# Another order of a recurrence's steps, with the second parts of its weights made on VectorE

## The chip, the cores and the metric

The kernel runs on one core of a Trainium2 chip. The core has TensorE (PE, matrix products; PEld is its loading of weights), VectorE (DVE), ScalarE (ACT), GpSimd (POOL) and SyncE (SP, which here issues DMAs), each with its own queue of instructions worked off in order. The metric is the device time of one execution in microseconds, the median of several runs.

## The reference

Two layers of a diffusion transformer on 512 latent and 256 context tokens (768 in all), width 1024. Layer 0 mixes by a gated linear recurrence, layer 1 by latent attention; each is followed by a SwiGLU feed-forward. The change lies in the mixer of layer 0:

```python
g, u = split(h @ w_in)                       # 1024 channels each
u = dwconv4(u) + b                           # along the tokens, one before and two after
for d, reverse in enumerate((False, True)):  # both directions
    r = sigmoid(blockdiag(u, gw[d, 0]) + gb[d, 0]);  i = sigmoid(blockdiag(u, gw[d, 1]) + gb[d, 1])
    a = exp(-8 * r * softplus(-lam[d]));  b = sqrt(1 - a**2) * (i * u)
    h_d = scan(a, b)                         # context first, then latent
x += mod * (((h_0 + h_1) * gelu(g)) @ w_out)
```

## The kernel before

Channels stand on the partitions and the 768 tokens along the free axis. Every float32 product is made of three rounded ones: `wh*xh`, `wh*xl` and `wl*xh`, where `wh` is the weight rounded and `wl` the rest (`mm3`, matmuls at L791).

The class `Stream` brings the weights. SP loads one into a `raw` buffer, of which there are two; ACT rounds it to `wh` (L108); a second instruction, here called its low, makes `wl = raw - wh` (L119) on the engine that `low_engine` names, which is GpSimd up to the end of the recurrence. A raw buffer comes free, and SP issues the next load, only after its last low. There are four `wh`/`wl` pairs. `done(i)` gives a pair back and calls `advance()`, which makes the lows still pending, splits the next unit, and leaves the low of the last one pending until the next `advance`, `flush` or `get` of that unit.

The recurrence goes through four blocks n of 256 channels, each in two halves. Its order is written by hand in `STEPS` (L296 to L304). Each step is a letter with n and further digits:

- `u`, `g`: input products (L791); `c`: convolution (ACT L895, six DVE instructions L899), then its split into `uh` (ACT L904) and `ul` (DVE L905); `G`: gelu (ACT L970).
- `t`, `T`: the two gate products of a direction and half (PE tiles `ga`) and their tanh (ACT L931).
- `e`: decays (DVE L941, three ACT instructions L948 to L950, DVE L951); `q`: square root (ACT L1037); `s`: the scan (DVE L956, then L958 and L959 forward, or L962 and the sum L964 backward).
- `m`: states times gelu (DVE L985), split into `mh` (ACT L986) and `ml` (DVE L988); `o`: an output tile (PE tiles `lo`) and its residual (DVE L767).
- `w`: `done` of the oldest used weight; `a`: a step of the modulation's products (PE `psada`, L570), whose DMAs POOL issues (L242).

The tiles `u`, `g`, `ga` and `lo` take turns in three PSUM buffers, so each of them waits until the tile three before it has been read. Names of steps carry digits: t201 is the gate product of block 2, direction 0, half 1. In the rows of the instruction order below, the tiles carry block, direction, half and gate: `ga2010` is t201, `ga2011` is T201, `lo2_4` is o24.

Of the kernel before, what the change touches and what calls it, by code (L numbers as in the profile page):

```python
# [145 lines left out]
def kernel(ctx, tc, x, c, ctx_in, c_ctx, ada_w, ada_b, norm_mix_g, norm_ffn_g, ffn_w_in,  # L146
# [3 lines left out]
    nc = tc.nc  # L150
    act, dve, pe = nc.scalar, nc.vector, nc.tensor
# [28 lines left out]
    def ps_main(name):  # L180
        return psstack[0][1].tile([P, 1024], F32, name=name, tag="main")
# [79 lines left out]
    st = Stream(nc, raw_pool, w_pool)  # L261
# [23 lines left out]
    def lru_gate_unit(n, d):  # L285
# [9 lines left out]

    STEPS = (  # L296
# [7 lines left out]
        "a g31 s311 w o20 o21 G30 o22 G31 w m3 w o23 o24 o25 o26 o27").split()  # L304

    g_units[0][0], = std_units(lru_w_in[0], 0, P)
    u_units[0] = [std_units(lru_w_in[0], D + i * P, P)[0] for i in range(2)]
# [200 lines left out]
    def ada_evac(wait=False):  # L508

        if ada_state["evac"] is None:  # L510
            return
        i, l, ch, sb = ada_state["evac"]
        if wait and ada_state["calls"] < 2:
            ada_state["calls"] += 1
            return
        ada_state["evac"] = None
        px = ps_aux(f"adax{i}")
        for cc in range(2):
            pe.transpose(px[:, cc * P:(cc + 1) * P], sb[:, cc * P:(cc + 1) * P], ident)

        order = "p (c j) -> p c j" if l and ch < 2 else "p (j c) -> p c j"
        n = dict(c=2, j=4)
        pv = px[:, :256].rearrange("p (c j r) -> p c j r", r=32, **n)
        for v in range(2):
            dve.tensor_tensor(mod[:, l, ch, v, :].rearrange(order, **n), pv[:, :, :, v],
                              adab(l, ch).rearrange(order, **n), op=ALU.add)
        if ch in (1, 4):
            w = l + (2 if ch == 4 else 0)
            for v in range(2):
                dve.scalar_tensor_tensor(gm[:, w, v, :], mod[:, l, ch, v, :], 1.0, gcol(w),  # L530
                                         op0=ALU.add, op1=ALU.mult)
# [12 lines left out]
    def ada_add():  # L544
        if ada_state["sums"] is None:
            return
        i, l, ch, half, total = ada_state["sums"]
        ada_state["sums"] = None
        if half == 0:
            ada_ps["half"] = psa.tile([P, 512], F32, name=f"psada{i}", tag="ada")  # L550
        ps = ada_ps["half"]
        for j in range(2):
            r = 64 * half + 32 * j
            pe.matmul(ps[r:r + 32, :256], pick[:, 0, :], total[:, j * 256:(j + 1) * 256], start=True, stop=True)
        if half == 1:
            ada_copy(i, l, ch, ps)
# [18 lines left out]
    def ada_one():  # L575
        ada_fill()
        i = ada_state["used"]
        l, ch, *f = adas[i]
        (ada_sum if l and ch > 1 else ada_product)(i, ada_tiles.pop(i), l, ch, *f)
        ada_state["used"] += 1  # L580
        ada_fill()

    def ada_step(n=1):

        if ada_state["sums"]:
            ada_state["calls"] += 1
            if ada_state["calls"] < 2:
                return
            ada_add()
        else:  # L590
            ada_evac(True)
        for _ in range(n):
            if ada_state["used"] < N_ADA[0] and not ada_state["sums"]:
                ada_one()
# [202 lines left out]
    def prod(ps, unit, xh, xl, parts, kt=KT, off=0, at=None):  # L797
        wh, wl = st.get(unit)
        for k in range(kt):
            if at and k in at:  # L800
                at[k]()
            mm3(ps, wk(wh, k), wk(wl, k), xh[:, k], xl[:, k], parts, k == 0, k == kt - 1, off)
# [118 lines left out]
    def gate(n, d, kk, g, uh, ul):  # L921

        wh, wl = st.get(gate_units[n][d])
        ps = ps_main(f"ga{n}{d}{kk}{g}")
        for k in range(2):
            o = (g * 2 + k) * 256 + kk * P
            mm3(ps, wh[:, o:o + P], wl[:, o:o + P], uh[:, k], ul[:, k], SL, k == 0, k == 1)
        tag, bufs = ("gel", 4) if (n, d, g) == (3, 1, 1) else (f"tg{g}", 4 - 2 * g)
        th = lt(f"tg{n}{d}{kk}{g}", tag, bufs)
        gi = (d * 2 + g) * 8 + 2 * n + kk  # L930
        act.activation(th, ps[:, :T], AF.Tanh, scale=0.5, bias=gbh[:, gi:gi + 1])  # L931
        gs["t", n, d, kk, g] = th
        if kk == g == 1:
            used.append(gate_units[n][d])

    def decay(n, d, kk, y):

        tr, ti = gs["t", n, d, kk, 0], gs["t", n, d, kk, 1]
        ci = d * 8 + 2 * n + kk
        cs = slice(ci, ci + 1)  # L940
        dve.scalar_tensor_tensor(ti, ti, 1.0, y, op0=ALU.add, op1=ALU.mult)  # L941
        if (n, d) == (3, 1):
            a = lt(f"a{n}{d}{kk}", "yc", 2)
        else:
            a = tmp.tile([P, T], F32, name=f"a{n}{d}{kk}", tag="nt")
        b = lt(f"b{n}{d}{kk}", "b", 1)
        gs["a", n, d, kk] = a
        act.activation(a, tr, AF.Exp, scale=m4[:, cs], bias=m4[:, cs])  # L948
        act.activation(b, tr, AF.Exp, scale=m8[:, cs], bias=m8[:, cs])
        act.activation(tr, tr, AF.Tanh, scale=p4[:, cs], bias=p4[:, cs])  # L950
        dve.scalar_tensor_tensor(tr, b, 1.0, tr, op0=ALU.add, op1=ALU.mult)  # L951

    def states(n, d, kk):

        a, b, ti = gs["a", n, d, kk], gs["t", n, d, kk, 0], gs["t", n, d, kk, 1]
        dve.tensor_tensor(b, b, ti, op=ALU.mult)  # L956
        if d == 0:
            dve.tensor_tensor_scan(b[:, CTXS], a[:, CTXS], b[:, CTXS], 0.0, op0=ALU.mult, op1=ALU.add)  # L958
            dve.tensor_tensor_scan(b[:, LAT], a[:, LAT], b[:, LAT], b[:, T - 1:T],  # L959
                                   op0=ALU.mult, op1=ALU.add)  # L960
        else:
            dve.tensor_tensor_scan(b[:, ::-1], a[:, ::-1], b[:, ::-1], 0.0, op0=ALU.mult, op1=ALU.add)  # L962
            f = gs["t", n, 0, kk, 0]
            dve.tensor_tensor(f, f, b, op=ALU.add)  # L964
# [3 lines left out]
    def gelu_of(n, kk, ps):  # L968
        ge = lt(f"gel{n}_{kk}", "gel", 4)
        act.activation(ge, ps[:, :T], AF.Gelu_apprx_tanh)  # L970
        gel[n, kk] = ge
        used.append(g_units[n][kk])
# [21 lines left out]
    def new_block(n):  # L994
        uc[n] = [lt(f"u{i}{n}", f"u{i}", 1, F32R, [P, 2, T]) for i in "hl"]
# [3 lines left out]
    def product(op, n, kk):  # L999
        pss[op, n, kk] = ps = ps_main(f"{op}{n}_{kk}")  # L1000
        prod(ps, (u_units if op == "u" else g_units)[n][kk], hh, hl, SL)

    def convolution(n, kk):
        ycs[n, kk] = conv(2 * n + kk, pss["u", n, kk])
        if kk == 0:
            new_block(n)
        conv_split(ycs[n, kk], *uc[n], kk)
        used.append(u_units[n][kk])

    new_block(0)  # L1010
    gelu_of(0, 0, p0[0])
    st.done(used.pop())
    ada_step()
# [6 lines left out]
    for op, *f in STEPS:  # L1020
        n, *f = map(int, f or "0")
        if op in "ug":
            product(op, n, *f)
        elif op == "c":
            convolution(n, *f)
        elif op == "G":
            gelu_of(n, *f, pss["g", n, *f])
        elif op in "tT":
            gate(n, *f, "tT".index(op), *uc[n])
        elif op == "w":  # L1030
            if used:
                st.done(used.pop(0))
        elif op == "e":
            decay(n, *f, ycs[n, f[1]])
        elif op == "q":
            b = gs["t", n, *f, 0]
            act.activation(b, b, AF.Sqrt, scale=0.25)  # L1037
        elif op == "s":
            states(n, *f)
        elif op == "m":  # L1040
            gated_states(n)
        elif op == "o":
            out_tile_of(n, *f, mts[n])
        else:
            ada_step()
    for i in used:
        st.done(i)
    ada_until(0, 5)
# [707 lines left out]
```

## Time and profile before

| | us |
|---|---|
| runs, median of 3 | 1565.74 (1564.92 to 1567.44) |
| profiled execution | 1566.9 |
| its span (first to last instruction) | 1565.1 |
| PE busy | 1510.2 (96%) |
| DVE, ACT, POOL busy | 936.8, 676.1, 260.3 |
| mean granted TensorE clock | 0.986 |

The span is what the profile covers; the profiled execution is 1.8 us longer than it. The recurrence lies between about 62 and 345 us. Lines are numbered as in the kernel before; a group of rows gives how many instructions it holds and their mean.

### The profile page before, as it was taken

To read this page: it belongs to the slowest core of one execution; us is meant where nothing else is said; L and a number is where in the kernel's file an instruction comes from. 1 tells how busy PE (TensorE), PEld (TensorE's weight loads), DVE (VectorE), ACT (ScalarE), POOL (GpSimd) and SP (SyncE) were. 2 spreads that over 40 slices of the span, in tenths; PEclk is the share of its full clock that TensorE was granted. 3 is DMA by queue.
4 is the path that set the end of the run, shared out by engine and by line. 5 is a ranking of instruction groups with operands and counts; after the bars stand their busy time and mean duration, and the time that the engine had idled before them with its cause. 6 is when DMAs were issued, how large, how long until landed. Compare 5 with 4: busy or idle time off the path is not lost.

```text
span 1565.1 us, 21623 instructions
## 1 busy us (share of the span) xinstructions
PE 1510.2 (96%) x8903; PEld 1320.1 (84%) x8903; DVE 936.8 (60%) x1407; ACT 676.1 (43%) x989; POOL 260.3 (17%) x251
## 2 busy tenths in 40 slices
PE   7999998979999999999999999999998999999998
PEld 5887876868879898999989887899998888888887
DVE  5765778687855666758677477665537543233234
ACT  5486555834323241433414344666644321232223
POOL 3223333252000101001010210111144100000002
PEclk8999999989999999999999999999999999999999
DMA  9334334131134334334332121110112432233222
GB/s 358 123 114 135 108 111 130 56 108 48 68 102 121 96 120 119 125 100 128 104 119 77 54 69 64 29 43 28 54 55 75 162 126 96 81 104 111 81 69 94
DMA packets 134995, 155.15 MB, mean 99 GB/s; under 512 B 6251, under 2 KB 112352, under 8 KB 134896
## 3 DMA queue, kind: packets, MB, share of 16 engines
q1 hardware_dynamic: 122272, 112.21, 22.1%
q0 software_dynamic: 12320, 41.02, 8.1%
q8 instruction: 70, 1.15, 0.3%
q10 hardware_dynamic: 304, 0.53, 0.1%
q14 instruction: 29, 0.24, 0.0%
HBM read 151.64 MB, written 2.10 MB: 98 GB/s over the span
## 4 chain that ended last, share of the span: by engine, by line
PE 83%; DVE 11%; ACT 4%; issue 1%; DMA 1%; SPq 0%; DVEq 0%; ACTq 0%
PE f L791 14%; PE fo L1212 12%; PE x L1166 10%; PE fo L791 8%; PE z L1166 5%; PE lo L791 3%; PE s L1553 3%; PE ga L791 2%; PE wo L791 2%; PE y L1166 2%; PE o L1595 2%; PE p L791 2%; PE g L791 2%; DVE yc L899 1%; PE t L1571 1%; DVE tg L962 1%
## 5 line engine op out<-in xcount | busy, mean ns | idle before, releaser
L108 ACT ACTIVATE wh<-raw 128x1024 fp32r<-128x1024 f32 (+3 forms) x247 | 208.4, 871 | 202.7 <-PE fo L1212 56.4
L119 POOL TENSOR_TENSOR wl<-raw,wh 128x1024 fp32r<-128x1024 f32 (+2 forms) x56 | 136.3, 2443 | 337.8 <-ACT wh L108 325.8
L119 DVE TENSOR_TENSOR wl<-raw,wh 128x1024 fp32r<-128x1024 f32 (+3 forms) x191 | 181.1, 961 | 18.7 <-ACT wh L108 18.5
L767 DVE SCALAR_TENSOR_TENSOR xT<-fo,mod,xT 128x512 f32<-128x512 f32 (+1 forms) x124 | 74.1, 626 | 127.6 <-PE fo L1212 64.6
L239 POOL DMA_DIRECT2D ada<-in_ada_w_dram x96 | 51.6, 537 | 465.4 <-PE psada L570 219.0
L791 PE MATMUL f<-hh,wh 128*128 128x512 f32 x320 | 124.7, 390 | 0.0
L791 PE MATMUL f<-hh,wl 128*128 128x512 f32 x320 | 124.5, 389 | 0.0
L791 PE MATMUL f<-hl,wh 128*128 128x512 f32 x320 | 124.5, 389 | 0.0
L785 POOL TENSOR_TENSOR acc<-acc,sq 128x256 f32<-128x256 f32 (+1 forms) x52 | 50.7, 974 | 381.0 <-ACT sq L783 379.9
L1212 PE MATMUL fo<-ah,wh 128*128 128x512 f32 (+1 forms) x352 | 98.3, 345 | 0.9 <-DVE g L1273 0.8
L1212 PE MATMUL fo<-al,wh 128*128 128x512 f32 (+1 forms) x352 | 95.8, 338 | 0.4 <-DVE al L1201 0.4
L1212 PE MATMUL fo<-ah,wl 128*128 128x512 f32 (+1 forms) x352 | 95.3, 337 | 0.0
L1109 DVE TENSOR_TENSOR sg<-sg,f 128x512 f32<-128x512 f32 x20 | 13.8, 688 | 116.3 <-ACT sg L1108 116.3
L1108 ACT ACTIVATE sg<-f 128x512 f32<-128x512 f32 x20 | 12.0, 599 | 147.9 <-PE f L791 147.9
L791 PE MATMUL fo<-ah,wh 128*128 128x512 f32 (+1 forms) x200 | 73.0, 365 | 0.0
L791 PE MATMUL fo<-ah,wl 128*128 128x512 f32 (+1 forms) x200 | 72.7, 364 | 0.0
L791 PE MATMUL fo<-al,wh 128*128 128x512 f32 (+1 forms) x200 | 72.7, 364 | 0.0
L791 PEld LDWEIGHTS f<-hh,wh 128*128 128x128 f32 x320 | 60.1, 188 | 13.3 <-issue 0.8
L791 PEld LDWEIGHTS f<-hh,wl 128*128 128x128 f32 x320 | 60.1, 188 | 12.4
L791 PEld LDWEIGHTS f<-hl,wh 128*128 128x128 f32 x320 | 60.1, 188 | 12.4
L1212 PEld LDWEIGHTS fo<-ah,wh 128*128 128x128 f32 x352 | 56.2, 188 | 12.9 <-issue 4.6
L1212 PEld LDWEIGHTS fo<-ah,wl 128*128 128x128 f32 x352 | 56.3, 189 | 7.8
(490 smaller groups left out, 4011.1 us busy)
## 6 DMA issues: line engine op xcount, KB each, us to landing
raw<-in_ffn_w_in_dram SPq DMA_DIRECT2D x26, 1024.0 KB, 4.9
ada<-in_ada_w_dram POOLq DMA_DIRECT2D x96, 256.0 KB, 3.0
raw<-in_ffn_w_out_dram SPq DMA_DIRECT2D x19, 1024.0 KB, 4.9
raw<-in_ffn_w_in_dram SPq DMA_DIRECT2D x36, 512.0 KB, 4.4
ada<-in_ada_w_dram POOLq DMA_DIRECT2D x30, 512.0 KB, 4.4
ada<-in_ada_w_dram SPq DMA_DIRECT2D x32, 256.0 KB, 5.5
raw<-in_lru_w_in_dram SPq DMA_DIRECT2D x10, 512.0 KB, 5.2
raw<-in_lru_gate_w_dram SPq DMA_DIRECT2D x16, 256.0 KB, 3.1
```

The costliest lines, as they stand in the source:

```text
L108: nc.scalar.activation(dst(hi), src(self.raw[load]), AF.Copy)
L119: self.low_engine.tensor_tensor(dst(lo), src(self.raw[load]), dst(hi).bitcast(F32), op=ALU.subtract)
L239: eng.dma_start(t, ada_w[l, k * P:(k + 1) * P, c0:c0 + 512])
L767: dve.scalar_tensor_tensor(xT[:, m, s], ps(s) if callable(ps) else ps[:, s], mod[:, l, ch, v, m:m + 1], xT[:, m, s], op0=ALU.mult, op1=ALU ...
L785: accs.append(lambda: nc.gpsimd.tensor_tensor(acc[:, s], acc[:, s], sq, op=ALU.add))
L791: pe.matmul(ps[:, off + s.start:off + s.stop], a, b[:, s], start=first and i == 0, stop=last and i == 2)
L899: dve.scalar_tensor_tensor(y[:, s0:s1], ps[:, s0 + o:s1 + o], convw(tap, k), y[:, s0:s1], op0=ALU.mult, op1=ALU.add)
L962: dve.tensor_tensor_scan(b[:, ::-1], a[:, ::-1], b[:, ::-1], 0.0, op0=ALU.mult, op1=ALU.add)
L1166: pe.matmul(ps, w[:, o:o + P], x[:, k0 + k, s], start=first and k == 0 and q == 0, stop=last and k == 3 and q == 2, skip_group_check=not f ...
L1212: pe.matmul(ps[v], w[:, o:o + P], x[:, k, s], start=k == 0 and q == 0, stop=k == nh - 1 and q == 2)
L1553: pe.matmul(ps[:, o:o + 384], x, y[:, k0:k1], start=j == 0, stop=j == 4)
L1595: pe.matmul(ps[:, :256], x[:, t % 4, hs], y[:, t, :], start=t == 0 and j == 0, stop=t == NT - 1 and j == 2)
```

## The change

Two things are changed. `STEPS` is rewritten in four places: c11 stands ahead of s011; o10 stands behind t201; a new token `f` (a flush of the pending lows) stands behind u30; and in the last block the out tiles o20 to o25 are spread between the gates, g30 and g31, while o27 stands last. Then `low_engine` is DVE from the first step to the end of the loop, and a counter `age` flushes a low that has been pending for four steps.

```diff
-        "e010 T011 e011 u10 q010 w a a s010 q011 c10 u11 w s011 a a w g11 c11 t100 w T100 m0 G11 w a a "
+        "e010 T011 e011 u10 q010 w a a s010 q011 c10 u11 w c11 s011 a a w g11 t100 w T100 m0 G11 w a a "
...
+        elif op == "f":
+            st.flush()
...
+
+        st.low_engine = dve
+        age = age + 1 if st.pending and op != "w" else 0
+        if age == 4:
+            st.flush()
+    st.low_engine = nc.gpsimd
```

Of the 30 lows that stood on POOL in the recurrence, 25 move to DVE; the first three and the last two stay. How the order moves shows in three places.

On DVE around the second convolution of block 1 (`yc3`, its split `ul1`) and the backward scan of block 0 (`tg0110`), the kernel before has:

```order
L905 TENSOR_TENSOR ul1_1178<-yc2_1169,uh1_1177 128x768
L956 TENSOR_TENSOR tg0110_1020<-tg0110_1020,tg0111_1085 128x768
L962 SCALAR_TENSOR_TENSOR tg0110_1020<-a011_1088,tg0110_1020 128x768
L964 TENSOR_TENSOR tg0010_899<-tg0010_899,tg0110_1020 128x768
L899 SCALAR_TENSOR_TENSOR yc3_1307<-u1_1_1181,cols_d_127,yc3_1307 128x511 x2
L899 SCALAR_TENSOR_TENSOR yc3_1307<-u1_1_1181,cols_d_127,yc3_1307 128x510
L899 SCALAR_TENSOR_TENSOR yc3_1307<-u1_1_1181,cols_d_127,yc3_1307 128x255 x2
L899 SCALAR_TENSOR_TENSOR yc3_1307<-u1_1_1181,cols_d_127,yc3_1307 128x254
L905 TENSOR_TENSOR ul1_1178<-yc3_1307,uh1_1177 128x768
L985 TENSOR_TENSOR gel0_0_751<-tg0000_867,gel0_0_751 128x768
```

The scan and its sum stood ahead of the convolution. In the changed kernel the same stretch of DVE reads:

```order
L905 TENSOR_TENSOR ul1_1181<-yc2_1172,uh1_1180 128x768
L899 SCALAR_TENSOR_TENSOR yc3_1236<-u1_1_1184,cols_d_127,yc3_1236 128x511 x2
L899 SCALAR_TENSOR_TENSOR yc3_1236<-u1_1_1184,cols_d_127,yc3_1236 128x510
L899 SCALAR_TENSOR_TENSOR yc3_1236<-u1_1_1184,cols_d_127,yc3_1236 128x255 x2
L899 SCALAR_TENSOR_TENSOR yc3_1236<-u1_1_1184,cols_d_127,yc3_1236 128x254
L905 TENSOR_TENSOR ul1_1181<-yc3_1236,uh1_1180 128x768
L956 TENSOR_TENSOR tg0110_1021<-tg0110_1021,tg0111_1089 128x768
L962 SCALAR_TENSOR_TENSOR tg0110_1021<-a011_1092,tg0110_1021 128x768
L964 TENSOR_TENSOR tg0010_899<-tg0010_899,tg0110_1021 128x768
L119 TENSOR_TENSOR wl10_1234<-raw9_1073,wh10_1233 128x1024
L119 TENSOR_TENSOR wl11_1266<-raw10_1170,wh11_1265 128x1024
L985 TENSOR_TENSOR gel0_0_751<-tg0000_867,gel0_0_751 128x768
```

The convolution now comes first, and two lows follow the scan; `wl10` is the second part of the weight that t100 uses.

On PE around block 2's first gates, here with the first row of each tile, the kernel before has:

```order
L791 MATMUL ga2000_1961<-uh2_1794,wh18_1818 128x512
...
L791 MATMUL ga2001_1978<-uh2_1794,wh18_1818 128x512
...
L791 MATMUL lo1_0_1996<-mh1_1936,wh19_1825 128x512
...
L791 MATMUL ga2010_2021<-uh2_1794,wh18_1818 128x512
...
L791 MATMUL lo1_1_2042<-mh1_1936,wh19_1825 128x512
...
L791 MATMUL ga2011_2057<-uh2_1794,wh18_1818 128x512
```

The out tile o10 stood between T200 and t201. In the changed kernel these tiles on PE are:

```order
L791 MATMUL ga2000_1964<-uh2_1794,wh18_1818 128x512
...
L791 MATMUL ga2001_1981<-uh2_1794,wh18_1818 128x512
...
L791 MATMUL ga2010_2006<-uh2_1794,wh18_1818 128x512
...
L791 MATMUL lo1_0_2021<-mh1_1936,wh19_1825 128x512
...
L791 MATMUL lo1_1_2045<-mh1_1936,wh19_1825 128x512
...
L791 MATMUL ga2011_2060<-uh2_1794,wh18_1818 128x512
```

Now t201 comes first, so it takes the PSUM buffer that o10 took, and T201 takes the one of t201.

On PE at the end of the recurrence, again with the first row of each tile, the kernel before has:

```order
L791 MATMUL ga3111_2623<-uh3_2285,wh25_2350 128x512
...
L791 MATMUL g3_0_2648<-hh0_78,wh26_2443 128x512
...
L791 MATMUL g3_1_2725<-hh0_78,wh27_2573 128x512
...
L791 MATMUL lo2_0_2777<-mh2_2497,wh28_2710 128x512
...
L791 MATMUL lo2_3_2846<-mh2_2497,wh28_2710 128x512
...
L791 MATMUL lo3_0_2936<-mh3_2832,wh30_2829 128x256
```

All eight out tiles of block 2 stood behind g31. In the changed kernel the end on PE reads:

```order
L791 MATMUL ga3111_2622<-uh3_2285,wh25_2350 128x512
...
L791 MATMUL lo2_0_2637<-mh2_2500,wh26_2443 128x512
...
L791 MATMUL lo2_3_2699<-mh2_2500,wh26_2443 128x512
...
L791 MATMUL g3_0_2714<-hh0_78,wh27_2573 128x512
...
L791 MATMUL lo2_4_2790<-mh2_2500,wh28_2696 128x512
...
L791 MATMUL g3_1_2823<-hh0_78,wh29_2776 128x512
...
L791 MATMUL lo2_6_2880<-mh2_2500,wh28_2696 128x512
...
L791 MATMUL lo3_0_2936<-mh3_2898,wh30_2787 128x256
```

Four out tiles now stand ahead of g30, two between g30 and g31, and two behind; the products of the last block (`lo3`) still come at the end.

## Rows read from the trace of the kernel before

**Rows 1.** The page's first part: busy us, share of the span, instructions.

```profile
PE 1510.2 (96%) x8903; PEld 1320.1 (84%) x8903; DVE 936.8 (60%) x1407; ACT 676.1 (43%) x989; POOL 260.3 (17%) x251
```

**Rows 2.** PE's waits, 62 to 345 us: us in total, times, longest.

```profile
PE lo L791 <- DVE xT L767: 8.3, 1, 8.3
PE ga L791 <- DVE yc L899: 5.1, 1, 5.1
PE lo L791 <- ACT tg L931: 3.0, 1, 3.0
PE ga L791 <- ACT uh L904: 3.0, 1, 3.0
PE ga L791 <- ACT tg L931: 1.4, 1, 1.4
PE ga L791 <- DVE ul L905: 0.4, 1, 0.4
```

**Rows 3.** Stretches behind waits: us; busy of each engine; granted clock; DMA share; GB/s.

```profile
132.20:135.60 3.40, 3.40 (x11) 2.92 (x12) 1.62 (x2) 1.97 (x3) 0.00 (x0) 0.50 0.00 0
...
237.30:240.70 3.40, 2.00 (x12) 1.73 (x12) 3.40 (x2) 3.25 (x5) 2.11 (x1) 1.00 0.39 135
272.10:278.90 6.80, 4.80 (x15) 4.15 (x16) 5.76 (x14) 3.65 (x4) 0.00 (x0) 0.50 0.30 106
323.30:333.50 10.20, 6.18 (x19) 5.31 (x20) 10.09 (x14) 3.20 (x4) 0.49 (x1) 0.50 0.19 67
```

**Rows 4.** POOL's groups, 62 to 345 us: busy, mean ns; idle before, releaser.

```profile
L119 POOL TENSOR_TENSOR wl<-raw,wh 128x1024 fp32r<-128x1024 f32 x30 | 80.0, 2672 | 79.8 <-ACT wh L108 79.6
```

**Rows 5.** DVE's groups, 62 to 345 us, the backward scan and its sum.

```profile
L962 DVE TENSOR_TENSOR_SCAN tg<-a,tg 128x768 f32<-128x768 f32 x8 | 20.4, 2544 | 0.3
L964 DVE TENSOR_TENSOR tg<-tg,tg 128x768 f32<-128x768 f32 x8 | 18.4, 2296 | 0.3
```

**Rows 6.** DVE's groups over the whole span, the lows made there.

```profile
L119 DVE TENSOR_TENSOR wl<-raw,wh 128x1024 fp32r<-128x1024 f32 x89 | 107.3, 1227 | 7.6 <-ACT wh L108 7.6
```

**Rows 7.** DVE's timeline before t100: start us, us, instruction.

```profile
119.61 3.88 DVE L962 TENSOR_TENSOR_SCAN tg<-a,tg 128x768 f32<-128x768 f32 x1
...
126.42 3.73 DVE L899 SCALAR_TENSOR_TENSOR yc<-u,cols_d,yc 128x511 f32<-128x511 f32 x6
```

**Rows 8.** PE's timeline, the third pair of matmuls of t100.

```profile
127.68 0.51 PE L791 MATMUL ga<-uh,wl 128*128 128x512 f32 x2
```

**Rows 9.** DVE's timeline, the states of block 1 times gelu.

```profile
206.37 4.44 DVE L985 TENSOR_TENSOR gel<-tg,gel 128x768 f32<-128x768 f32 x2
```

**Rows 10.** ACT's timeline, the tanh of t200, T200 and t201.

```profile
213.00 0.90 ACT L931 ACTIVATE tg<-ga,gbh 128x768 f32<-128x768 f32 x1
...
215.92 0.90 ACT L931 ACTIVATE tg<-ga,gbh 128x768 f32<-128x768 f32 x1
...
221.99 0.88 ACT L931 ACTIVATE tg<-ga,gbh 128x768 f32<-128x768 f32 x1
```

**Rows 11.** DVE's timeline before t301.

```profile
263.04 0.96 DVE L964 TENSOR_TENSOR tg<-tg,tg 128x768 f32<-128x768 f32 x1
...
264.91 1.76 DVE L962 TENSOR_TENSOR_SCAN tg<-a,tg 128x768 f32<-128x768 f32 x1
266.70 3.60 DVE L964 TENSOR_TENSOR tg<-tg,tg 128x768 f32<-128x768 f32 x1
```

**Rows 12.** DVE's timeline in the last block.

```profile
310.77 3.84 DVE L962 TENSOR_TENSOR_SCAN tg<-a,tg 128x768 f32<-128x768 f32 x1
314.65 2.98 DVE L964 TENSOR_TENSOR tg<-tg,tg 128x768 f32<-128x768 f32 x1
...
326.13 3.24 DVE L767 SCALAR_TENSOR_TENSOR xT<-lo,mod,xT 128x512 f32<-128x512 f32 x6
```

**Rows 13.** ACT's groups, 62 to 345 us, the copies to `wh`.

```profile
L108 ACT ACTIVATE wh<-raw 128x1024 fp32r<-128x1024 f32 x29 | 29.9, 1047 | 9.6 <-PE lo L791 6.7 <-DMA raw<-in_lru_w_out_dram 2.9
```

**Rows 14.** DMA issues, 100 to 345 us: count, KB each, median us to landing.

```profile
raw<-in_lru_w_out_dram SPq DMA_DIRECT2D x8, 512.0 KB, 3.8
```

More of the change, by code (lines that the diff above doesn't have):

```diff
@@ L297 @@
         "g01 a t000 w G01 T000 t001 w e000 T001 a g10 e001 G10 a q000 s000 q001 a t011 t010 w s001 a T010 "
[1 row of a table removed]
[1 row of a table added]
         "t101 e100 T101 e101 q101 g20 q100 G20 w a o00 t110 T110 t111 T111 w a a s101 s100 o01 o02 e111 "
         "o03 o04 o05 o06 q111 e110 w s111 o07 w a u20 c20 a a q110 s110 w w u21 c21 g21 m1 a a t200 G21 "
[3 rows of a table removed]
-        "a g31 s311 w o20 o21 G30 o22 G31 w m3 w o23 o24 o25 o26 o27").split()
[3 rows of a table added]
+        "w s310 G30 w o24 s301 o25 g31 s311 G31 o26 w m3 o27 w").split()
     g_units[0][0], = std_units(lru_w_in[0], 0, P)
@@ L1010 @@
     new_block(0)
+    age = 0
     gelu_of(0, 0, p0[0])
```

6 rows, old and new, of the table STEPS are left out of this document.

## The prediction

> **What bounds the kernel now.** I read the page's first part, then PE's waits in the recurrence, then the granted clock behind each wait, then the DVE and ACT timelines that end those waits. PE is busy for 1510.2 of 1565.1 us [rows 1], so time comes back only where PE stands still or runs slowly. Between 62 and 345 us PE waits 21.2 us in six waits [rows 2], at four places: A, t100 (3.0 + 0.4, for the split of c11); B, o10 (3.0, for a tanh) and soon after it T211 (1.4, for a tanh); C, t301 (5.1, for c31); D, o23 in the last block (8.3, for a residual on DVE). Behind a wait there is a second price. Right after A, C and D the granted clock is 0.50, the lower level of 1.2 GHz, for stretches in which PE is busy for 3.40, 4.80 and 6.18 us; the stretch after B's long wait (214.1 to 217.5) is like A's. Behind the 1.4 us wait (237.3 to 240.7) it stayed 1.00 [rows 3]. At half clock half of the busy time is lost: (3.40 + 3.40 + 4.80 + 6.18) / 2 = 8.9 us. So 21.2 + 8.9 = 30.1 us is all that this change can find in the recurrence; the order behind it is not touched.
>
> **The lows on DVE.** POOL makes 30 lows at a mean of 2.67 us [rows 4]; 25 of them become DVE's. Elsewhere the same instruction takes DVE 1.23 us [rows 6], so DVE gains 25 x 1.23 = 30.7 us of work. But DVE is also slowed today: the backward scan L962 takes 1.76 us in one block and 3.84 to 3.88 in others, its sum L964 0.96 or up to 3.60 [rows 7, 11, 12]. The two groups together would give back 20.4 - 8 x 1.76 + 18.4 - 8 x 0.96 = 17.0 us if every one were as short [rows 5, 11]. I read these stretches as instructions that stand still while POOL makes a low.
>
> The trace's long and short forms of one instruction bear on a rule: the Trainium skill, "SBUF — State Buffer", section "Who interferes with whom", says that a DVE instruction with two inputs in SBUF and a GpSimd instruction that reads SBUF exclude each other, and the loser blocks fully. By the rule alone each of the 25 lows could hold DVE for its whole 2.67 us, 66.8 us; by the rows of the scan and its sum the return is 17.0 us. The trace agrees on the kind; on the size the rows stand.
>
> The bounds of a moved low on the path are 1.23 us [rows 6] and 2.67 us (POOL's own [rows 4]), and below nothing where the low ends earlier than POOL's would. I take 1.23, since nothing on POOL reads with it any more.
>
> **Place A.** Before, DVE runs the scan from 119.61 and its sum, and c11 only from 126.42 to 130.15 [rows 7]. Now c11 comes first: it starts where the product ahead of the scan did (119.61 - 0.96 = 118.65, with L964's short form for a product of the same shape) and ends at 122.4; ACT's copy to `uh` (1.05, as the copies in [rows 13]) and `ul` (0.96) are through at 124.4, and the 3.4 us of waiting go. But `wl10` now stands on DVE behind the scan: 124.4 + 0.96 + 1.76 + 0.96 + 1.23 = 129.3. t100 wants it in its third pair, which started at 127.68 [rows 8]: a new wait of 1.6. A later low also frees its raw buffer later, and the load behind it takes 3.8 us [rows 14]; the copy that needs it stands ahead of a tanh in ACT's queue, for which I put 0.55 at g20. New waits 2.15.
>
> **Place B.** `m1` takes 4.44 us for two products [rows 9], where 2 x 0.96 would do by L964's short form: 2.5 earlier. So the tanh of t200, ended at 213.90 [rows 10], comes 2.5 earlier, less about 0.6 for a low that now stands ahead of c21. t201 now takes the PSUM buffer o10 waited for: 3.0 - 2.5 + 0.6 = 1.1. T201 then needs the buffer of t201, whose tanh stands on ACT behind a copy, a table load and three exponentials. From the end of T200's tanh (216.82) to the end of t201's (222.87) that took 6.05 us [rows 10], and T200's ended 216.82 - 213.90 = 2.92 after t200's: 8.97 in all. PE has t201, o10, o11 and a piece of modulation to fill it, 3 x 2.1 + 0.6 = 6.9 (a tile is six pairs of 0.35). New wait 2.1. The 1.4 of T211 goes, because its tanh is no later while PE is. New waits 3.2.
>
> **Place C.** The path to c31 holds 1.76 for the scan, which is short here already, and the sum at 3.60 [rows 11]; the scan before it was stretched by 3.84 - 1.76 = 2.1 [rows 11, 12]. 5.1 - 2.1 - (3.60 - 0.96) + 1.23 for `wl24` leaves 1.6; I take 1.9, since residuals of o14 and o15 queue in the same stretch, and two of 0.45 behind it. New waits 2.8.
>
> **Place D.** The out tiles o20 to o22 stood behind g31, and their residuals on DVE behind the scans, which fill it from 310.77 to 326.13 at least [rows 12]. Now o20 to o23 run ahead of g30, so their residuals stand ahead of the scans, and g30 and g31 (48 matmuls each) cover the scans. Of stretching 3 x 2.0 go, the scan and its sum (3.84 - 1.76, 2.98 - 0.96) [rows 11, 12] and the next scan taken as alike. Four lows come in, 4 x 1.23 = 4.9. What is late next is a row of short things: T311's tanh before o22 (0.9), `wl28` before o24 (0.75), `wl29` before g31 (0.55), the split of `m3` before the last block's first product (1.85), a residual behind `wl31` (1.2), and the first norm, whose sums stand on POOL behind the two lows that stay there (1.0). New waits 6.3.
>
> **Edits I cost at nothing.** `f` puts the low for o14 ahead of c30 on DVE. c30 is then 1.23 late, and t301, its first reader, comes behind u31 (24 pairs, 8.4 us) and four out tiles (8.4); without that cover it would cost 1.23. SP's loads and POOL's modulation DMAs keep their order, and POOL only gets freer.
>
> **The sum.** Waits 21.2 before, 2.15 + 3.2 + 2.8 + 6.3 = 14.45 after: -6.75. Clock: none of the new waits is as long as 3 us; the 1.4 us wait cost no clock [rows 3] and those of 3.0 did. Some between fall in: I take two stretches of 3.4 us busy, 3.4 lost, against 8.9: -5.5. Together -12.25. The span of 1565.1 becomes 1552.85, the execution with its 1.8 outside 1554.65. The profiled execution is 1.16 above the median of the runs, so 1553.5. With no drop the gain is 15.65; with four of 1.7 each it is 8.8. If my new waits are off by 2 to 3 in sum, the likeliest case's own range is a gain of 6 to 17, that is 1549 to 1560. The chance is 0.70.
>
> **Rivals.** First, that many short waits pull the clock down as the few long ones did. For it: eight of my new waits are 0.9 us or longer, some close together. Against it: the 1.4 us wait [rows 3]. With seven such stretches, 7 x 1.7 = 11.9 against 8.9, the clock turns into a loss of 3.0 and the gain is 6.75 - 3.0 = 3.7: 1562. The Trainium skill, "TensorE: Matmul & The Clock Gate", section "A second HAM failure mode: psum-queue depth-cycling", tells of a kernel whose short idles between groups of matmuls made the clock go back and forth. By that rule this rival would be the likely one; the one short wait that the trace shows in the recurrence speaks against it. The chance is 0.11.
>
> Second, slower: a low that waits for up to four steps in DVE's queue frees its raw buffer late. A step is (345 - 62) / 192 = 1.5 us, so four are 5.9 us, less 2.67 - 1.23 = 1.4 that the instruction is shorter: the next load is issued up to 4.5 us later, and it takes 3.8 [rows 14]. ACT works in order, so a copy that comes before its data holds each tanh behind it, and with it PE. ACT's copies wait 2.9 us in all for a load today, for one of 29 [rows 13], which speaks for slack. If the slack is short by 1.0 us at some 19 of the 25, the time is 1553.5 + 19 = 1572. It decides where a copy comes before the landing of its load. The chance is 0.08.
>
> Third, that the change does not do what it should: if the long scans are not POOL's doing, DVE gets 30.7 us of work and nothing back, and three or four lows stand ahead of the waits that DVE ends (A, C and D), 3.5 x 1.23 = 4.3: 1565.7 + 4.3 = 1570. For it: I have not tied each long form to a low of POOL. Against it: L964 has two clear sizes. The chance is 0.03.
>
> Fourth, more than forecast: the new waits at A, B and D stay under what the PSUM buffers cover, with -18 to -21: 1545 to 1548. The chance is 0.08.
>
> **How the numbers follow.** The range is 1547 to 1562: it leaves out the two slower cases (0.11), half of the clock's (0.05) and half of the fourth (0.04). What a measurement of this kernel tells from no change is 0.2%, 3.1 us. Faster by more: 0.70 + 0.08 + 0.06 of the clock's case = 0.84. Within it: the clock's other 0.05 and 0.01 at the edge = 0.06. Slower: 0.10.
>
> **What would show it.** In the profile after: L962 at about 1.8 and L964 at about 1.0 us throughout (else the third rival); no wait for `uh` at t100, but one of 1 to 2 us for a low; at T201 a wait for a tanh of about 2; at t301 under 3; no single wait over 3 in the last block; the clock at 0.50 in at most four short stretches. Copies on ACT that wait for loads by more than 15 us in sum would be the second rival, and more than 9 us lost at half clock the first. The prediction is wrong if the waits in the recurrence stay above 21 us.

## The result and the profile after

The changed kernel takes 1552.48 us (median of 4 runs, 1551.79 to 1554.86), against 1565.74 us before: a ratio of 0.9922, with a 95% interval of 0.9908 to 0.9937. The forecast was 1553.5. The profiled execution has a span of 1553.1 us. One execution of a later kernel (e5) took 5023.72 us, over three times the others, and is left out of that kernel's time.

The page's first part, after (as [rows 1]):

```profile
PE 1508.5 (97%) x8903; PEld 1317.4 (85%) x8903; DVE 927.8 (60%) x1432; ACT 676.5 (44%) x989; POOL 193.4 (12%) x226
```

DVE has 25 instructions more and is 9 us less busy: the lows it took over weigh less than the stretches it lost. PE's waits from 62 to 345 us, after (as [rows 2]: us in total, times, longest):

```profile
PE ga L791 <- ACT tg L931: 2.4, 3, 1.6
PE lo L791 <- DVE xT L767: 2.1, 1, 2.1
PE ga L791 <- DVE yc L899: 1.4, 1, 1.4
PE R_f0a L662 <- DVE dg_f0a L656: 1.2, 1, 1.2
PE ga L791 <- DVE wl L119: 1.2, 1, 1.2
PE lo L791 <- DVE ml L988: 0.9, 2, 0.6
PE lo L791 <- ACT mh L986: 0.6, 1, 0.6
PE g L791 <- ACT gel L970: 0.4, 1, 0.4
PE g L791 <- DVE wl L119: 0.2, 1, 0.2
PE ga L791 <- DVE ul L905: 0.2, 1, 0.2
```

The sum is 10.6 us, against 21.2 in [rows 2], and no wait is over 2.1. The two windows aren't quite alike: the whole recurrence is shorter now, so the wait of the first norm (`R_f0a`) falls inside the window, while before it lay behind 345 us, with another 0.2 for its sums:

```profile
PE R_f0a L662 <- DVE dg_f0a L656: 0.8, 1, 0.8
```

With these it was 22.2 us before against 10.6 now. The stretches at half clock, after (as [rows 3]: us, busy time of each engine, granted clock), the first in the last block's products, the second at the start of the feed-forward:

```profile
328.60:332.00 3.40, 3.40 (x18) 3.40 (x17) 1.45 (x3) 1.24 (x4) 3.16 (x5) 0.50 1.01 343
...
352.40:359.20 6.80, 6.80 (x32) 6.76 (x32) 3.71 (x10) 0.85 (x3) 0.39 (x1) 0.51 0.75 253
```

Of the four stretches of before (three in [rows 3] and the one at place B) one is left in the recurrence, 3.4 us long. The second stands behind a wait of 1.8 us that both kernels have at the first products of the feed-forward, behind the first norm. Before, the stretch behind that wait was half as long:

```profile
367.60:371.00 3.40, 3.40 (x18) 3.40 (x18) 2.31 (x8) 0.20 (x1) 0.00 (x0) 0.51 0.53 180
```

DVE's groups from 62 to 345 us, after (as [rows 5, 6]):

```profile
L119 DVE TENSOR_TENSOR wl<-raw,wh 128x1024 fp32r<-128x1024 f32 x25 | 31.7, 1273 | 3.0 <-ACT wh L108 3.0
...
L962 DVE TENSOR_TENSOR_SCAN tg<-a,tg 128x768 f32<-128x768 f32 x8 | 14.1, 1758 | 0.3
...
L964 DVE TENSOR_TENSOR tg<-tg,tg 128x768 f32<-128x768 f32 x8 | 7.7, 958 | 0.3
```

Every backward scan now has the short form, 1.76 us, and every sum 0.96: 17.0 us came back in these two groups alone (20.4 - 14.1 + 18.4 - 7.7), as the prediction had it.

Where the span's 12.0 us went is read from three marks on PE's timeline (start us, us, instruction): the recurrence's first product, the feed-forward's first, and the feed-forward's third pair of tiles. Before, then after:

```profile
62.01 0.50 PE L791 MATMUL g<-hh,wh 128*128 128x512 f32 x1
...
360.00 0.28 PE L791 MATMUL f00g<-hh,wh 128*128 128x256 f32 x1
...
399.95 0.50 PE L791 MATMUL f02g<-hh,wh 128*128 128x512 f32 x1
```

```profile
63.48 0.50 PE L791 MATMUL g<-hh,wh 128*128 128x512 f32 x1
...
346.33 0.28 PE L791 MATMUL f00g<-hh,wh 128*128 128x256 f32 x1
...
387.85 0.50 PE L791 MATMUL f02g<-hh,wh 128*128 128x512 f32 x1
```

From the first mark to the second it took 298.0 us and takes 282.9: 15.1 less. From the second to the third it took 39.95 and takes 41.5: 1.6 more, which is the longer stretch at half clock. Ahead of the first mark this execution is 1.5 later, which the change doesn't touch. -15.1 + 1.6 + 1.5 = -12.0.

Place A stands on DVE's timeline, after (as [rows 7]), as the order said:

```profile
119.99 3.75 DVE L899 SCALAR_TENSOR_TENSOR yc<-u,cols_d,yc 128x511 f32<-128x511 f32 x6 [0.95 <-ACT yc L895]
...
126.58 1.76 DVE L962 TENSOR_TENSOR_SCAN tg<-a,tg 128x768 f32<-128x768 f32 x1
128.37 0.96 DVE L964 TENSOR_TENSOR tg<-tg,tg 128x768 f32<-128x768 f32 x1
129.25 2.35 DVE L119 TENSOR_TENSOR wl<-raw,wh 128x1024 fp32r<-128x1024 f32 x2
```

The convolution is early, and the low that t100 needs (the first of the two) is ready only at about 130.4, behind the scan and its sum. A low that is late also frees its raw buffer late, and as the prediction had it, a copy to `wh` that stands ahead of a tanh waits for a load, with g20's 0.4 behind it (in e14, where the low comes earlier, neither waits):

```profile
134.78 1.06 ACT L108 ACTIVATE wh<-raw 128x1024 fp32r<-128x1024 f32 x1 [1.65 <-DMA raw<-in_lru_w_out_dram]
```

### The profile page after: what moved, and what is told of

The parts are those of the page before. It is cut to its first block, busy times and chain, and to the rows that moved or that the text cites. A ratio compares the mean times of both kernels' runs of the same rounds, so it can differ in the third digit from the quotient of the medians.

```text
span 1553.1 us, 21602 instructions
## 1 busy us (share of the span) xinstructions
PE 1508.5 (97%) x8903; PEld 1317.4 (85%) x8903; DVE 927.8 (60%) x1432; ACT 676.5 (44%) x989; POOL 193.4 (12%) x226
## 4 chain that ended last, share of the span: by engine, by line
PE 77%; issue 9%; DVE 8%; ACT 3%; DMA 2%; POOL 0%; DVEq 0%; SPq 0%; POOLq 0%; ACTq 0%
PE f L791 14%; PE fo L1221 12%; PE x L1175 10%; PE fo L791 8%; PE z L1175 5%; PE s L1562 3%; PE wo L791 2%; PE y L1175 2%; PE o L1604 2%; DMA ada<-in_ada_w_dram 2%; PE t L1580 1%; DVE xT L767 1%; PE ckv L791 1%; DVE wl L119 1%; PE p L791 1%
## 5 line engine op out<-in xcount | busy, mean ns | idle before, releaser
L119 DVE TENSOR_TENSOR wl<-raw,wh 128x1024 fp32r<-128x1024 f32 (+2 forms) x216 | 212.8, 997 | 21.6 <-ACT wh L108 21.4
L119 POOL TENSOR_TENSOR wl<-raw,wh 128x1024 fp32r<-128x1024 f32 (+2 forms) x31 | 69.6, 2258 | 302.4 <-ACT wh L108 262.1
L791 PEld LDWEIGHTS f<-hh,wl 128*128 128x128 f32 x320 | 60.1, 188 | 12.6
L1221 PEld LDWEIGHTS fo<-al,wh 128*128 128x128 f32 x352 | 56.2, 188 | 8.0 <-DVE al L1210 0.7
```

The costliest lines, as they stand in the source:

```text
L119: self.low_engine.tensor_tensor(dst(lo), src(self.raw[load]), dst(hi).bitcast(F32), op=ALU.subtract)
L791: pe.matmul(ps[:, off + s.start:off + s.stop], a, b[:, s], start=first and i == 0, stop=last and i == 2)
L1221: pe.matmul(ps[v], w[:, o:o + P], x[:, k, s], start=k == 0 and q == 0, stop=k == nh - 1 and q == 2)
```

## The experiments

The time moved as forecast, but the prediction gave three parts one account: the order, the engine of the lows, and the flush at age four. The runs take them apart. Each ratio is against the kernel before on the same chip in the same series. The new order holds `f`. Theory 1 was that the end of DVE's stretching makes most of the gain and the order the rest.

| order | lows on | flush at 4 | us (median) | ratio, 95% interval |
|---|---|---|---|---|
| before | POOL | no | 1565.7 | 1 |
| before | POOL | yes | 1557.3 | 0.9953 (0.9936 to 0.9969) |
| new | POOL | no | 1565.6 | 0.9999 (0.9990 to 1.0008) |
| new | POOL | yes | 1552.5 | 0.9925 (0.9911 to 0.9938) |
| before | DVE | yes | 1558.6 | 0.9963 (0.9950 to 0.9975) |
| before, with f | DVE | yes | 1551.6 | 0.9920 (0.9905 to 0.9935) |
| new | DVE | no | 1568.5 | 1.0020 (1.0009 to 1.0031) |
| new (the change) | DVE | yes | 1552.5 | 0.9922 (0.9908 to 0.9937) |

**The order of before** (e1). `STEPS` is that of before in all its places, of which one is shown; engine and flush are as changed.

```diff
-        "e211 w u30 f e210 c30 q210 w o14 ...
+        "e211 w u30 e210 c30 q210 w o14 ...
...
```

> The order of before, with the lows on VectorE and the flush at age four (no f). Theory 1 (most of the gain is the end of VectorE's stalls beside GpSimd, the order adds a part, mostly in the last block): t301's wait falls from 5.1 to about 1.5, those for c11 from 3.4 to about 1, o10's from 3.0 to about 1, but o23's stays at 3 to 7; about 1556 us (1553 to 1560). Rival a (the order does it): 1562 or more. Rival b (the order adds nothing): 1552.5.

It took 1558.62 us. The waits from 230 to 345 us:

```profile
PE lo L791 <- DVE wl L119: 11.0, 2, 7.2
PE lo L791 <- DVE xT L767: 1.9, 1, 1.9
```

The time is in Theory 1's range, the reason isn't. t100 and t301 don't wait at all. Instead o14 waits 7.2 us for its low, which stands behind c30 on DVE: c30 is the third step behind the w, and the flush comes at the fourth. A second wait for a low, 3.8 us, stands in the last block. The first is what `f` is for, and it was forecast at nothing.

**The lows back on GpSimd** (e2), order and flush as changed.

```diff
-        st.low_engine = dve
```

> The new order with f and the flush at age four, but every low back on GpSimd. Theory 1: the long forms of the scan and its sum come back (means above 2.2 us each for L962 and L964), t301 still waits about 5 and the clock falls behind it; what the order gives at t100 and in the last block stays in part: about 1560 us (1557 to 1563). Rival a (the order does it): 1553. Rival b (the order adds nothing): 1566.

It took 1552.52 us, ratio 0.9925: as fast as the change. Theory 1 falls. The long forms are there, if fewer (DVE's groups, 62 to 340 us):

```profile
L962 DVE TENSOR_TENSOR_SCAN tg<-a,tg 128x768 f32<-128x768 f32 x8 | 18.2, 2276 | 0.3
L964 DVE TENSOR_TENSOR tg<-tg,tg 128x768 f32<-128x768 f32 x8 | 13.9, 1734 | 0.3
```

PE hardly waits for them any more. So what counts here is less how long DVE is stretched than at which instruction.

**c11 back** (e3): one token of the change undone.

```diff
-        ... c10 u11 w c11 s011 a a w g11 t100 ...
+        ... c10 u11 w s011 a a w g11 c11 t100 ...
```

> The changed kernel with c11 back behind g11, all else as changed. With the scan at 1.8 and its sum at 1.0 us the convolution would end at about 126 anyway, as t100 comes up: theory 1 expects a wait of about 1 us for uh in place of the 1.2 us for the low, and 1552 to 1554 us. Rival (the place of c11 carries what was gained at t100, as the working of place A has it): the waits of 3.4 us and a stretch at half clock are back, 1556 to 1558 us.

It took 1547.11 us, ratio 0.9893 (0.9880 to 0.9907): below Theory 1's range and the rival's, and about 5 us below the change. DVE's timeline before t100:

```profile
117.79 1.76 DVE L962 TENSOR_TENSOR_SCAN tg<-a,tg 128x768 f32<-128x768 f32 x1
119.58 0.96 DVE L964 TENSOR_TENSOR tg<-tg,tg 128x768 f32<-128x768 f32 x1
120.46 1.22 DVE L119 TENSOR_TENSOR wl<-raw,wh 128x1024 fp32r<-128x1024 f32 x1
121.59 3.74 DVE L899 SCALAR_TENSOR_TENSOR yc<-u,cols_d,yc 128x511 f32<-128x511 f32 x6
```

With a short scan in DVE's idle time, both the low and the convolution come in time, and PE has no wait ahead of t200. How much of the 5 us this is comes with e14.

**The last block back** (e5): from T311 on the order of before.

```diff
-        ... t311 a e310 T311 o20 o21 a e311 q300 q310 o22 q311 w o23 g30 ...
+        ... t311 a e310 a T311 e311 q300 q310 q311 g30 q301 s300 s310 s301 w w a g31 ...
```

> The changed kernel with the order of before from T311 on. Theory 1: o23 waits again for a residual behind the scans, now without their stretching, 4 to 6 us instead of 8.3, with a stretch at half clock behind it: 1555 to 1558 us. Rival (the waits in the last block were only VectorE's stalls): 1552 to 1553 us.

It took 1555.15 us, ratio 0.9940 (0.9926 to 0.9953), at the lower end of Theory 1's range. The longest wait is 3.9 us, but for a low of an out weight, not for a residual; 1.8 for a residual follow. So the new order of the last block is worth some 2.7 us by the medians and 1.7 by the profiles, from the recurrence's first product to the feed-forward's; the intervals overlap, so this is not clear of noise.

These runs gave Theory 2: the order and the engine do the same work twice at c11 and c31, and with lows on DVE each low needs its place.

**The order of before with f** (e7), engine and flush as changed. Against the order of before:

```diff
-        "e211 w u30 e210 c30 ...
+        "e211 w u30 f e210 c30 ...
```

> The order of before with only the token f added, lows on VectorE and the flush at age four. Theory 2 (the order and the engine do the same work twice: each alone ends the lines at c11 and c31, and the lows on VectorE need f, since without it o14's low stands behind c30, 7.2 us plus a stretch at half clock): the 9.3 us lost at o14 go, about 1.5 to 4 come at t301, so 1550 to 1554 us. Rival (f is not what it hung on): 1557 to 1560 us.

It took 1551.61 us, as Theory 2 had it: 7 us less than e1 by one token. With it the order of before does as well as the change, so the rest of the new order nets nothing on DVE. That what it may gain in the last block is spent at c11 is argued from e3 and e5, not shown by itself.

**c11 and o10 back** (e8): c11 as in e3, and o10:

```diff
-        "T200 w e200 t201 o10 a o11 ...
+        "T200 o10 w e200 t201 a o11 ...
```

> The changed kernel with c11 and o10 both where they stood before. Theory 2: T201's wait for the tanh of t201 (1.6) goes and o10 waits about 0.5, since m1's products are short now; about 1.5 us below the kernel with c11 alone put back: 1544 to 1547 us. Rival (the move of o10 gains, as place B of the prediction had it for the wait of 3.0): 1549 us or more.

It took 1548.29 us, ratio 0.9898 (0.9884 to 0.9911), beside 0.9893 for e3. It is between Theory 2's range and the rival's. T201's wait is gone and o10 waits 0.6, as Theory 2 had it, and on PE's timeline u30 begins 168.2 us behind the recurrence's first product, against 170.1 in e3. So o10's move costs about 2 us there. The whole time doesn't show it: e8's profile has two stretches at half clock further on that e3's hasn't, behind the same waits (last section).

**GpSimd and c11 back** (e9).

```diff
-        ... c10 u11 w c11 s011 a a w g11 t100 ...
+        ... c10 u11 w s011 a a w g11 c11 t100 ...
...
-        st.low_engine = dve
```

> The new order with all lows on GpSimd (as e2_pool_lows), but c11 back behind g11. Theory 2: here the move of c11 is needed, since the scan and its sum have their long forms: the waits for uh and ul (3.3) and a stretch at half clock come back at t100, about 4 to 5 us above e2_pool_lows: 1556 to 1558 us. Rival (c11's move costs with either engine): 1547 to 1552 us.

It took 1559.59 us, ratio 0.9970 (0.9958 to 0.9981), 7 us above e2 and above Theory 2's range. Its waits up to 150 us:

```profile
PE ga L791 <- ACT uh L904: 3.3, 1, 3.3
PE ga L791 <- DVE ul L905: 0.4, 1, 0.4
```

So c11's move is a gain while POOL makes the lows and a loss when DVE makes them. By the medians it is 7 and 5 us. On PE's timeline, from the recurrence's first product to the out tile o00, it is 4.4 (89.5 here, 85.1 in e2) and 2.1 (85.9 in the changed kernel, 83.8 in e3); what the medians have beyond that is not tied to c11.

**No flush at age four** (e10), engine and order as changed.

```diff
-        if age == 4:
+        if age == 100:
```

> The changed kernel without the flush at age four: a low now waits for the next step w, for f or for its first use. Theory 2: loads are issued later, ScalarE's copies wait for them somewhat longer than the 5.2 us in all of the changed kernel, and a few lows come just as they are used: 1552 to 1557 us. The prediction's second rival (late raw buffers hold up ScalarE and with it TensorE): copies wait over 15 us in all, 1560 us or more.

It took 1568.50 us, ratio 1.0020 (1.0009 to 1.0031): far above Theory 2's range and near the 1572 of the prediction's second rival. Its waits from 62 to 350 us, and ACT's copies:

```profile
PE g L791 <- DVE wl L119: 5.3, 2, 2.8
PE ga L791 <- DVE wl L119: 3.4, 2, 2.2
...
PE u L791 <- DVE wl L119: 0.5, 1, 0.5
```

```profile
L108 ACT ACTIVATE wh<-raw 128x1024 fp32r<-128x1024 f32 x29 | 30.2, 1049 | 12.6 <-DMA raw<-in_lru_w_out_dram 10.2 <-DMA raw<-in_ffn_w_in_dram 2.4
```

The copies wait 12.6 us for loads, against 5.2 in the changed kernel, under the 15 that rival asked for; PE waits 9.2 us for lows themselves, against 1.4. So it is the low that comes late, more than its raw buffer. That waits of the copies need not cost is seen in e7, which took 1551.61 us:

```profile
L108 ACT ACTIVATE wh<-raw 128x1024 fp32r<-128x1024 f32 x31 | 32.2, 1048 | 17.1 <-DMA raw<-in_lru_w_out_dram 13.0 <-DMA raw<-in_ffn_w_in_dram 3.4 <-PE lo L791 0.8
```

There they wait over 15 us for loads, the sign that the prediction gave for its second rival, and the time is that of the change. The flush is worth 16 us here.

**One low moved** (e14): a flush behind c11 in the changed kernel. On DVE `wl10` alone moves, to ahead of the scan.

```diff
-        ... c10 u11 w c11 s011 a a w g11 t100 ...
+        ... c10 u11 w c11 f s011 a a w g11 t100 ...
```

> The changed kernel with one token more, f behind c11: on VectorE wl10 alone moves, from behind the backward scan and its sum to ahead of them. Theory 2 (c11's move costs with lows on VectorE because wl10 stands behind the scan, nothing else): t100's wait of 1.2 for the low goes to nothing and g20's 0.4 stays or shrinks: about 1.5 to 2 us below the changed kernel, 1549.5 to 1552 us. Rival (the 5 us between the changed kernel and the one with c11 back are something else, such as the clock): t100's wait goes, but the time stays at 1552.5 or more, or the wait stays.

It took 1549.03 us, ratio 0.9900 (0.9883 to 0.9917), half a microsecond below Theory 2's range. DVE before t100:

```profile
124.90 1.22 DVE L119 TENSOR_TENSOR wl<-raw,wh 128x1024 fp32r<-128x1024 f32 x1
...
127.03 1.76 DVE L962 TENSOR_TENSOR_SCAN tg<-a,tg 128x768 f32<-128x768 f32 x1
```

Neither t100 nor g20 waits any more, so there it was the low's place. The first product of o00 shows what it is worth, in the changed kernel and here:

```profile
149.36 0.50 PE L791 MATMUL lo<-mh,wh 128*128 128x512 f32 x1
```

```profile
146.57 0.50 PE L791 MATMUL lo<-mh,wh 128*128 128x512 f32 x1
```

The recurrence's first product begins at 63.48 and 62.80, so o00 comes after 85.9 and 83.8 us: 2.1 less, and 83.8 is also what e3 has. In all the recurrence is 3.4 us shorter here (279.4 against 282.9). The other 1.3 lies further on, where the last stretch at half clock is missing, behind the same wait of 2.1 us for a residual. e8 has that stretch and e3 hasn't, so it is not shown to be the low's doing.

**Late lows at the end** (e12), with c11 back: `wl31` behind the first residual of the last block, and the two lows that had stayed on POOL made on DVE.

```diff
-    st.low_engine = nc.gpsimd
-    for i in used:
-        st.done(i)
     ada_until(0, 5)
     for m in range(KT):
...
             st.flush()
+        if m == 3:
+            for i in used:
+                st.done(i)
```

The last w of `STEPS` is left out with it.

> c11 back, and at the end of the recurrence the last low of an out weight (wl31) behind the first residual of the last block, and the two lows that stayed on GpSimd made on VectorE between later residuals. Theory 2: the wait of 2.1 us for a residual behind wl31 (which takes 2.6 us there beside GpSimd's low) goes, and with it the stretch at half clock if there is one: 1544.5 to 1547 us. Rival (the wait moves on to the first norm): 1547 to 1549 us, with over 2 us of waits at the norm.

It took 1550.68 us, ratio 0.9915 (0.9897 to 0.9933): a miss, above both ranges, and if anything worse than e3. Its waits from 316 to 350 us:

```profile
PE lo L791 <- DVE xT L767: 1.5, 1, 1.5
PE f01g L791 <- DVE xT L767: 1.0, 1, 1.0
PE R_f0a L662 <- DVE dg_f0a L656: 0.9, 1, 0.9
```

The wait of 2.1 became one of 1.5, the norm still waits about 1 (0.7 and 0.3 in e3), and one of 1.0 is new at the feed-forward's first products. So it moved on, as the rival said, though not to over 2 us at the norm. Most of the difference from e3 in the profiles, 2.6 us, lies at the start of the feed-forward: that wait, and 3.4 us at half clock that e3 hasn't (last section).

**The flush alone** (e13): order of before, lows on POOL. Of the change this is left:

```diff
+        age = age + 1 if st.pending and op != "w" else 0
+        if age == 4:
+            st.flush()
```

> The order of before and all lows on GpSimd, with only the flush at age four added. Theory 2 (on GpSimd the order is what gains; when a low is queued there hardly matters): the waits at t100, o10, t301 and o23 stay near 3, 3, 5 and 8 us: 1562 to 1567 us. Rival (the flush is what gained in the run with the new order and GpSimd): 1552 to 1556 us.

It took 1557.30 us, between the two: the flush alone gives 8.4 us. It moves single lows of POOL. DVE's `m1` products, and the sum and convolution of c31, in this kernel:

```profile
206.43 1.82 DVE L985 TENSOR_TENSOR gel<-tg,gel 128x768 f32<-128x768 f32 x2
...
262.98 0.96 DVE L964 TENSOR_TENSOR tg<-tg,tg 128x768 f32<-128x768 f32 x1
263.86 3.74 DVE L899 SCALAR_TENSOR_TENSOR yc<-u,cols_d,yc 128x511 f32<-128x511 f32 x6
```

and POOL's timeline at the same places:

```profile
196.18 7.01 POOL L119 TENSOR_TENSOR wl<-raw,wh 128x1024 fp32r<-128x1024 f32 x2 [4.57 <-ACT wh L108]
...
263.57 2.61 POOL L119 TENSOR_TENSOR wl<-raw,wh 128x1024 fp32r<-128x1024 f32 x1
```

Before, POOL had a low beside `m1`:

```profile
207.56 2.42 POOL L119 TENSOR_TENSOR wl<-raw,wh 128x1024 fp32r<-128x1024 f32 x1
```

The products of [rows 9] took 4.44 us beside it and take 1.82 now, and o10's wait falls from 3.0 to 0.4. The low that had stretched the sum ahead of c31 to 3.60 [rows 11] now runs beside the convolution, which has one of its two inputs in PSUM and keeps its 3.74; t301 waits 2.2 instead of 5.1. The waits at t100 and o23 stay (3.3 and 8.1). An earlier load is not the reason: ACT's copies wait 2.7 us for loads, against 2.9 before. The Trainium skill, "SBUF — State Buffer", section "Who interferes with whom", says that a DVE instruction with at most one input in SBUF, outside its two-port modes, does not contend with GpSimd. These rows agree, and this is the use of the rule here that I had missed: a low need not leave GpSimd, it can be queued beside such an instruction.

That is Theory 3.

**The order alone** (e15): new order with f, lows on POOL, no flush.

```diff
-        st.low_engine = dve
...
-        if age == 4:
+        if age == 1000:
```

> The new order with its f, all lows on GpSimd, and no flush at age four. Theory 3 (on GpSimd the flush gains by moving single lows beside a convolution, whose input is in PSUM and which isn't stretched, and away from m1's products and from the sum ahead of c31): the 4.4 us pair of L985 and the sum of 3.6 us come back, with waits of about 3 at t201 and 4 to 5 at t301 and half clock behind them, while c11 and the last block keep what the order gives: 1557 to 1562 us. Rival (the order alone makes the gain): 1552 to 1554 us.

It took 1565.60 us, ratio 0.9999: above the range of Theory 3, far from the rival. The wait at c11 is gone, that at t201 is back (3.0, with half clock behind it), t301 waits 2.3, and a new one stands in the last block (waits from 280 to 340 us):

```profile
PE g L791 <- DVE xT L767: 5.3, 1, 5.3
```

A product in the last block waits 5.3 for a residual on DVE. That the new last block loses without the flush what c11's move gains is argued from these waits, not tested alone. Theory 3 had the mechanism at t201, and not the last block; at t301 the sum kept its short form, 0.96, so there it was wrong: with the new order the low stands beside the convolution without the flush.

## Why the prediction was right, and where its reasons were not

**Waits.** The forecast was -6.75, and -10.6 came in the same window; with the first norm's wait on both sides, which the prediction took for new, it is -11.6 (22.2 to 10.6). Place A: 1.6 behind `wl10` and 0.55 at g20 forecast, 1.2 and 0.4 measured. Place B: 1.1 and 2.1 forecast, 0.5 and 1.6 measured, and T211's wait went. Place C: 1.9 and twice 0.45 forecast; 1.4 and 0.2 measured, and 0.3 at T311, further on. Place D: 6.3 forecast, 5.0 measured; o22 and `wl28` didn't wait (0.9 and 0.75 forecast), the split of `m3` cost 1.5 instead of 1.85, but the residual behind `wl31` 2.1 instead of 1.2. The prediction gave each moved low 1.23 us, as nothing on POOL would read with it any more. For `wl31` that is wrong: it runs beside the two lows that stayed on POOL, and takes near the upper bound of 2.67:

```profile
324.63 2.60 DVE L119 TENSOR_TENSOR wl<-raw,wh 128x1024 fp32r<-128x1024 f32 x1
```

But for those two in place D, the waits stood about where they were put; the sum was too large by a third (14.45 against 10.6).

**Clock.** The forecast was -5.5, for the recurrence. There 8.9 lost at half clock became 1.7, which is -7.2; at the start of the feed-forward, where nothing was forecast, 1.7 became 3.4. Waits and clock of the recurrence together (-11.6 - 7.2 = -18.8) are 3.7 more than the 15.1 between the marks. Half of the busy time is somewhat too much: before, PE's pairs of matmuls start 0.64 us apart behind t100's wait and 0.35 at full clock, so 45% was lost, which takes 0.7 off the 7.2. There are 13 waits now instead of 8, and a slower first pair of matmuls behind a wait (0.61 us instead of 0.51 at t100) may hold part of what is left. The cause of the rest, up to 3 us, stays open.

So that the time came within 1 us of the forecast is in part luck: the waits fell by some 4 to 5 us more than forecast, and the clock at the feed-forward's start and the open rest took that back.

**The step that failed.** Right as a sum, the account had a wrong cause: it held that the waits at B and C go because the lows leave POOL. e2 and e13 show the same waits small with every low on POOL. What they need is that no low stands beside the few DVE instructions that PE waits for, and the flush alone does that at B and C (o10 waits 0.4 in e13, t301 2.2). Nor is it enough to leave POOL: without the flush (e10) the change is no gain. The prediction's place A was right that `wl10` would be late, but took c11's move for the gain and the low for its price; with short scans the move has nothing to gain (e3), only the price, 2.1 us up to o00 (e14). And `f`, costed at nothing, is worth 7 us on DVE in the order of before (e7 against e1); it was not taken out of the new order.

**The rivals.** The clock's rival did not come: of the short waits in the recurrence only the last, 2.1 us, has a stretch at half clock behind it, and the longer stretch at the feed-forward's start stands behind a wait that both kernels have. The second rival had about the size of what the flush prevents (1572 forecast, 1568.5 measured in e10), with the low itself late more than the load. The third falls, as L962 and L964 are short throughout. The fourth's 1545 to 1548 wasn't the change's, but one token away from it (e3, 1547.1), and that version is faster than both kernels.

## What to carry to other kernels

When VectorE's instructions show two clear durations, look for which of them are on a path and which GpSimd instruction stands beside just those; queueing that one a few steps earlier, beside an instruction with an input in PSUM, can give as much as moving all of them: with the new order it did (1552.5 us either way). When work is moved into an engine's in-order queue, each piece needs a place ahead of its first reader, and a rule that bounds its age needs a hand where the steps are long. Two edits that end the same wait don't add, so measure each without the other: here one of them, c11's move, was a loss once the other was in.

## What the runs showed of the hardware that I had not expected

All fourteen kernels have the same wait of 1.8 us at the feed-forward's first products. It was followed by 3.4 us at half clock before and in e12, 6.8 us in the changed kernel and ten others, and none in e3, where a window over it has the full clock:

```profile
343.00:360.00 17.00, 15.23 (x99) 13.49 (x98) 15.38 (x27) 6.97 (x12) 3.65 (x5) 1.00 0.32 109
```

From the feed-forward's first product to its third pair of tiles it took 38.4 us in e3's profile, 39.95 before, and 41.3 to 41.6 in the eleven with 6.8 us at half clock, for the same stretch of code. The last block is alike: behind the same wait of 2.1 us for a residual the changed kernel and e8 have a stretch at half clock, e3 and e14 none. One profile of each can't tell whether this is the kernel's or the execution's. But one kernel's executions differ too: of e3's four, two have a mean granted clock of 0.996 and two 0.994, and 0.002 of its span is about 3 us. So a difference of up to some 3 us between versions is read here only as far as PE's timeline shows where it arises.
